# Making the first tile's last expert queries inside its own gather stage, with their weights kept for the second tile

## The chip, the cores and the metric

One Trainium2 chip; the kernel runs on one of its cores. The metric is the device time of one execution in microseconds. The engines are called PE (TensorE), VectorE (DVE in the profile), ScalarE (ACT), GpSimd (POOL) and SP (SyncE, which only issues transfers here).

## The reference, cut to what matters

A decoder trunk of four layers on 256 tokens of width 1024, all in float32. Each layer is a token mixer (HGRN2, FoX attention, Mamba-2 SSD, HGRN2 again) and then an expert layer called PEER. The mixers are causal, so the second half of the tokens needs the first.

```python
for i in range(DEPTH):                       # 4
    h = h + mixer_i(rmsnorm(h, norm_mix[i]))
    h = h + peer_ffn(rmsnorm(h, norm_ffn[i]), ...)
out = rmsnorm(h, norm_final)

def peer_ffn(h, w_q, sub_keys, u_tab, v_tab):    # blocks of 128 tokens
    q = (xb @ w_q).reshape(128, 8, 2, 128)               # 8 heads, w_q is 1024 x 2048
    s = einsum('mhcd,hckd->mhck', q, sub_keys)           # 2 x 128 scores a head
    # the 16 best of each half, then the 16 best of their 256 sums: 16 of 16384 experts a head
    u, v = u_tab[idx], v_tab[idx]                        # rows of 1024
    act = gelu(einsum('md,mhkd->mhk', xb, u)) * softmax(top_s)
    return einsum('mhk,mhkd->md', act, v)
```

Each token reads 8 x 16 rows of u and of v, so 256 tokens and 4 layers read 1.07 GB of expert rows.

## The kernel before, in words

**Gathers.** The tokens form two tiles of 128. The expert layer of one layer and one tile is a *stage*; there are eight, stage s = 2 x layer + tile. A stage has 64 *pairs* (8 heads x 8). For one pair GpSimd issues two indirect gathers (`fetch`, L1389), each of 128 rows of u and v side by side, 1 MB, into one buffer of 2048 columns. VectorE then multiplies and sums the u half (`dot`), ScalarE forms the gated weight on a diagonal (`gated`, `active`; tile `dg`), and PE adds the weighted v half into the stage's sums (`spread`, L1457; tile `acc`). Then `given_back` returns the two buffers to `ring`, and the next pair's `fetches` issue gathers into whatever `ring` holds.

**Side work.** While stage s gathers, everything that stage s+1 needs is made beside it (`side`, `ready`): the norm, the mixer of the next tile (`hgrn`, `fox`, `ssd`), and the queries and scores of its eight heads (`queries`). So an even stage makes the second tile's mixer of its own layer, and an odd stage the first tile's mixer of the next layer. In each pair the main loop runs one step of the side work after `spread` (`products_`), paced by `SIDE[s]`. Top-16 selection (`route`, VectorE) runs some steps a pair, a few heads ahead of the gathers. What comes before the first gather is called the prelude.

**Weights.** A unit is 1 MB, [128 x 2048]. The program walks through `stream`, the list of all units in the order of use: a mixer's units (20 for HGRN2, 16 for FoX, 32 for SSD), then the eight of the query matrix (`wq0` to `wq3`), for each tile. `loads` issues them on SP's queue in the order of `order`, into one of three raw tiles (`raw`), or into a place of its own (`homes`, used once at the start), or, for units named in `KEEP`, into one of six *kept places* in the tile `arena`. A kept unit is loaded for the first tile and used again for the second.

**Places and gather buffers are one pool.** There are seven gather buffers (`NGB`), and a kept place that holds no unit circulates in `ring` as an eighth to thirteenth. When a kept unit comes due, `look_ahead` asks for its place, and the next pair that gives this buffer back makes it vacant. After the second tile has used a kept unit, its place goes back to `ring`.

**What sets the order.** All engines run their instructions in the order in which the program writes them; the waits are semaphores. A gather waits until the buffer's last reader, PE's weighted sum, is done. A raw load waits until PE has used the raw tile's former unit.

The scores of a tile's eight heads stand in `SS` (2048 columns), 256 columns a head.

Of the kernel before, what the change touches and what calls it, by code (L numbers as in the profile page):

```python
# [11 lines left out]
F32 = mybir.dt.float32  # L12
# [22 lines left out]

KEEP = {"hg": (1, 4, 7, 10, 14, 18), "fox": (1, 3, 5, 7, 9, 11, 14), "ssm": (1, 4, 8, 13, 18, 25)}
NKEPT = 6
# [5 lines left out]

SIDE = (43.3, 34.6, 37.5, 100, 100, 38.6, 38.4, 1.8)
SPAN = 56
# [125 lines left out]
def trunk(ctx: ExitStack, tc: tile.TileContext, d: dict, out: bass.AP):  # L171
# [94 lines left out]

    stream = []
# [6 lines left out]
    homes = {3: GB[0], 17: GB[0], 18: GB[1], 19: GB[2], 20: GB[3], 21: GB[4], 22: GB[5], 23: GB[6],  # L274
             27: mix[:, D:3 * D], 28: mix[:, SPACE:SPACE + UNIT], 30: mix[:, 3 * D:5 * D]}
    order = [0, 1, 2, "rest", *range(3, 10), 22, 10, 11, 12, 23, 13, 14, 15, 16, "x", 17, 20, 18, 21, 19, "keys",
             "factors", 28, 29, 24, "heads", 27, 25, 26, "states"]
    order += range(30, len(stream))
    over = set()
# [6 lines left out]
    def spot(u):  # L286

        if isinstance(u, str):
            return None
        nm, i = stream[u]  # L290
        p = KEEP.get(nm.rstrip("01"), ())
        k = p.index(i) if i in p else len(spots)
        return k if k < len(spots) and (nm, i) not in kept else None

# [25 lines left out]
    def loads():  # L320

        while order:
# [12 lines left out]
            else:  # L335
                nm, i = stream[u]
                places = KEEP.get(nm.rstrip("01"), ())
                keep = i in places
                if keep:
                    k = places.index(i)  # L340
# [27 lines left out]
    def half(nm, use):  # L368

        u, k = divmod(pos[1], 2)  # L370
# [11 lines left out]
    def project(nm, ub, names):  # L382

        for key in names:
            b = pjp.tile([P, 512], F32, name="pj")
            for k in range(4):
                def use(w):
                    for c in range(2):
                        mm(b, xT[:, 2 * k + c], w[:, c], 2 * k + c == 0, 2 * k + c == DC - 1)
                half(nm, use)  # L390
                if k == 3:
                    ub[key] = b
                yield
# [35 lines left out]
    class Plan:  # L429
        def __init__(self):  # L430
            self.slots = {}

        def pe(self, n, f, *a):
# [33 lines left out]

    def weighed(row, q, b):

        c = slice(4 * q, 4 * q + 4)  # L470
        tm(xT[:, c], b, weights[:, 8 * row + 4 * q:8 * row + 4 * q + 4].unsqueeze(2).to_broadcast([P, 4, P]), op=OP.mult)

    def half_turned(row, e):

        turned(h[:, 0, e * 512:(e + 1) * 512], lambda b: weighed(row, e, b))

# [11 lines left out]
    def normed(t, acc, row, xn, alone=False):  # L488
# [44 lines left out]
        if not last:  # L533
            yield from slot(*(lambda q=q: turned(xn[:, es[q]], lambda b: weighed(row, q, b)) for q in range(2)))


    def hgrn(l, t, carry):
# [179 lines left out]
        for q in range(2):  # L717
# [14 lines left out]
            else:  # L732
# [56 lines left out]
    def fox(l, t, carry):  # L789
# [93 lines left out]
        for j in range(8):  # L883
# [3 lines left out]
            p.pe(n + 2, scores_turn, j)  # L887
            p.pe(n + 3, out_heads, j)
        p.halves([16, 17, 21, 22], out_project("fox", [YT[:, i] for i in range(8)], acc))
        yield from p.run(3.0)  # L890
# [3 lines left out]
    def ssd(l, t, carry):  # L894
# [223 lines left out]
        for j, n in enumerate([24, 26, 29, 31]):  # L1118
            p.pe(n, gates_turn, j)
            p.pe(n + 1, group_norm, j)  # L1120
            p.at(n + 1, group_root, j)
            p.at(n + 2, group_scale, j)
        gen2 = out_project("ssm", [XT[:, i] for i in range(16)], acc)
        for n in [31, 32, 33, 34] * 3 + [35, 36] * 2:
# [8 lines left out]
    scored, got, routed = set(), {}, [0]  # L1133

    def queries(s, carry):

        l = s // 2
        ub = {}
        top[0] = FREE[KIND[l]]
# [11 lines left out]
        def score(g):  # L1151
            assert s == 0 or routed[0] > 8 * (s - 1) + 2 * g + 1, (s, g, routed)
            b = bank()
# [8 lines left out]
        def alone():  # L1162
# [4 lines left out]
            for hh in range(2):  # L1167
                e, c = slice(hh * 256, hh * 256 + 256), slice(2 * hh, 2 * hh + 2)

                def products(ks):  # L1170
                    for k in ks:
                        mm(b[:, e], xT[:, k], ws[k // 4][:, k % 4, e], k == 0, k == DC - 1)
                if hh == 0:
# [31 lines left out]
        for n, _ in enumerate(p.run(99)):  # L1205
            yield

            while n % 2 and s and routed[0] < min(8 * s, 8 * s - 6 + len([1 for k in scored if k[0] == s])):
                yield "wait"
# [16 lines left out]
    def route(s, hh):  # L1226
# [14 lines left out]
        ig = wk2.tile([P, 2, TOPK], F32, name="ig")  # L1241
        yield from top16([(sv[:, c], si[:, c], SS[:, hh, c]) for c in range(2)])
        vec.tensor_copy(sf, si)
# [124 lines left out]

    def repeated():

        todo = []
        for g in range(2):
            for e in range(2):
                b = bank()
                for c in range(4):
                    for j in range(2):
                        mm(b[j * 64:j * 64 + 64, c * P:(c + 1) * P], xT[:, 4 * e + c, g * 64:g * 64 + 64], ident, True, True)
                todo.append((XR[:, g, e * 512:(e + 1) * 512], b))
# [152 lines left out]
    next(routing)  # L1531
    for i, (o, b) in enumerate(repeated()):
        act(o, b, AF.Copy, scale=rts[1][:, 3 + i // 2:4 + i // 2])
# [14 lines left out]
    for s in range(STAGES):  # L1548
# [26 lines left out]
        for i in range(64 * s, 64 * s + 64):  # L1575
# [15 lines left out]
            if end:  # L1591
                (_, b), (o, c) = x[2:]
                nc.scalar.copy(x[2][0], b)
                vec.tensor_copy(o, c)
            route_steps(3, i // 8 + 3)
            others()
            products_()
            if i % 64 == 62 and s + 1 < STAGES:
# [3 lines left out]
                others()  # L1602
                x = repeated()
            if i == len(pairs) - 1:
# [24 lines left out]
```

## Time and profile before

| | |
|---|---|
| time, median of 3 runs | 3189.3 us (3189.02 to 3190.45) |
| the profiled execution's own time | 3190.3 us |
| its span | 3188.5 us |
| PE, VectorE, ScalarE, GpSimd busy | 82%, 66%, 48%, 39% of the span |
| bytes moved | 1309.40 MB, of which gathers 1073.81 MB |
| unit loads of query weights | 64 (59 into raw tiles, 5 into `arena`), 1 MB each |
| gathers | 1028 |

The chain of waits follows the work back from the last instruction. Releasers are read from semaphores; where the same helper line (L209 for VectorE, L222 for ScalarE, L247 for PE) serves many operations, the tile's name tells which one it is: `pj` are products with weights, `ps` small products and transposes, `acc` the stage's sums.

### The profile page before, as it was taken

How to read it: one execution, taken by the hardware profiler on the slowest of the kernel's cores; microseconds unless marked ns; L12 is line 12 of the kernel's file. 1: busy time of each engine (PE TensorE's matmuls, PEld its weight loads, DVE VectorE, ACT ScalarE, POOL GpSimd, SP SyncE). 2: the span in 40 equal slices, each digit the busy share in tenths (PEclk: the TensorE clock that was granted, in tenths of full speed). 3: DMA queues.
4: the chain of work that ended last, by engine and by line, in shares of the span. 5: the costliest groups of instructions: out<-in, count | busy, mean ns of one | idle time of the engine just before them, and what ended most of it. 6: DMA issues, size and time to landing. Idle time of an engine off the chain costs nothing.

```text
span 3188.5 us, 31234 instructions
## 1 busy us (share of the span) xinstructions
PE 2630.3 (82%) x8618; PEld 973.5 (31%) x8618; DVE 2114.4 (66%) x5602; ACT 1544.0 (48%) x4403; POOL 1231.8 (39%) x1034
## 2 busy tenths in 40 slices
PE   9889877787788886989878998788887888876666
PEld 4433232232233322334323343222322323221111
DVE  1577747676677756778567886476665767667765
ACT  3454434364345543577335784354443554343343
POOL 0244433343344434333334333342333444444544
PEclk9999988998999998999999999999999999999989
DMA  7899999999999999999999999999999999999997
GB/s 314 357 421 421 421 421 421 400 412 421 420 420 420 421 421 421 419 391 398 421 418 413 421 420 421 421 420 415 393 421 412 420 421 421 421 421 421 421 420 322
DMA packets 181500, 1309.40 MB, mean 411 GB/s; under 512 B 20176, under 2 KB 20688, under 8 KB 22608
## 3 DMA queue, kind: packets, MB, share of 16 engines
q0 software_dynamic: 147776, 1073.81, 81.4%
q1 hardware_dynamic: 33552, 233.59, 17.7%
q8 instruction: 72, 1.18, 0.1%
q14 instruction: 100, 0.82, 0.1%
HBM read 1306.27 MB, written 1.05 MB: 410 GB/s over the span
## 4 chain that ended last, share of the span: by engine, by line
DMA 61%; PE 13%; issue 9%; DVE 8%; ACT 4%; POOL 3%; POOLq 0%; SPq 0%; DVEq 0%; ACTq 0%
DMA arena<-in_uv,ix 61%; DVE arena L209 6%; PE pj L247 5%; PE acc L1457 5%; POOL arena L1389 3%; PE ps L247 2%; ACT L222 1%; ACT dg L222 1%; ACT arena L222 1%; PE ps L251 1%; DMA arena<-in_hg 0%; DVE eq L209 0%; ACT dots L222 0%; DVE si L209 0%; DVE ti L209 0%
## 5 line engine op out<-in xcount | busy, mean ns | idle before, releaser
L1389 POOL DMA_INDIRECT arena<-in_uv,ix x1028 | 1229.7, 1196 | 1939.6 <-PE acc L1457 869.5
L209 DVE SCALAR_TENSOR_TENSOR arena<-arena 128x1024 f32<-128x1024 f32 (+3 forms) x1280 | 1320.1, 1049 | 887.2 <-DMA arena<-in_uv,ix 877.1
L1457 PE MATMUL acc<-arena,dg 128*64 128x512 f32 x4096 | 1458.7, 666 | 534.1 <-ACT dg L222 528.8
L222 ACT ACTIVATE dots<-dots 128x1 f32<-128x1 f32 x1024 | 203.8, 199 | 1368.9 <-DVE arena L209 1368.4
L1457 PEld LDWEIGHTS acc<-arena,dg 128*64 128x64 f32 x4096 | 354.3, 145 | 1460.1 <-ACT dg L222 1061.6
L247 PE MATMUL pj<-raw,arena 128*128 128x512 f32 x1440 | 673.3, 610 | 4.2 <-DVE arena L209 3.2
L222 ACT ACT_TABLE_LOAD x322 | 413.1, 1283 | 7.6 <-DVE fst L209 1.3
L247 PEld LDWEIGHTS pj<-raw,arena 128*128 128x128 f32 x1440 | 262.2, 192 | 411.9 <-issue 387.7
L222 ACT ACTIVATE dg<-dg,dots 128x64 f32<-128x64 f32 x1024 | 356.1, 348 | 33.2
L222 ACT ACTIVATE dg<-m,gs 128x64 f32<-128x64 f32 x1024 | 293.9, 335 | 0.0
L247 PE MATMUL pj<-arena 128*128 128x512 f32 (+1 forms) x496 | 222.2, 591 | 0.2
L247 PE MATMUL ps<-arena 128*128 128x128 f32 (+3 forms) x992 | 131.3, 287 | 1.6 <-ACT arena L1187 1.0
L247 PEld LDWEIGHTS pj<-arena 128*128 128x128 f32 x496 | 90.0, 191 | 126.6 <-issue 122.3
L247 PEld LDWEIGHTS ps<-arena 128*128 128x128 f32 (+2 forms) x992 | 102.3, 167 | 68.0 <-issue 44.6
L251 PE MATMUL ps<-fst,arena 128*128 128x128 f32 x568 | 90.9, 286 | 9.1 <-DVE arena L209 5.2
L251 PEld LDWEIGHTS ps<-fst,arena 128*128 128x128 f32 x568 | 66.8, 145 | 87.7 <-issue 45.5
L222 ACT ACTIVATE arena<-arena 128x512 f32<-128x512 f32 (+3 forms) x132 | 67.7, 554 | 52.7 <-DVE arena L209 50.6
L209 DVE DVE_READ_ACCUMULATOR arena<-arena 128x1 f32 x1024 | 84.9, 83 | 0.0
L209 DVE FIND_INDEX8 si<-sv,arena 128x8 uint32<-128x128 f32 x256 | 69.8, 285 | 0.0
L247 PE MATMUL ps<-cst,arena 128*128 128x128 f32 (+3 forms) x288 | 66.6, 358 | 0.0
L209 DVE MAX8 sv<-arena 128x8 f32<-128x128 f32 x256 | 61.7, 283 | 3.4 <-ACT arena L1191 3.4
L222 ACT ACTIVATE arena<-ps 128x512 f32<-128x512 f32 (+3 forms) x114 | 43.3, 426 | 25.7 <-PE ps L247 25.2
(129 smaller groups left out, 1257.6 us busy)
## 6 DMA issues: line engine op xcount, KB each, us to landing
raw<-in_wq SPq DMA_DIRECT2D x59, 1024.0 KB, 9.1
raw<-in_ssm SPq DMA_DIRECT2D x52, 1024.0 KB, 9.2
raw<-in_hg SPq DMA_DIRECT2D x50, 1024.0 KB, 9.3
raw<-in_fox SPq DMA_DIRECT2D x18, 1024.0 KB, 9.2
arena<-in_hg SPq DMA_DIRECT2D x17, 1024.0 KB, 13.6
arena<-in_uv,ix POOLq DMA_INDIRECT x1028, 19.1
arena<-in_fox SPq DMA_DIRECT2D x7, 1024.0 KB, 13.8
arena<-in_ssm SPq DMA_DIRECT2D x6, 1024.0 KB, 14.3
```

The source lines that it names most:

```text
L209: return getattr(nc.vector, name)(o, *a, **k)
L222: nc.scalar.activation(o, i, f, **k)
L247: nc.tensor.matmul(o, w, m, start=start, stop=stop)
L251: nc.tensor.transpose(o, i, ident)
L1389: nc.gpsimd.indirect_dma_start(o, None, src, bass.IndirectOffsetOnAxis(ap=ix, axis=0))
L1457: nc.tensor.matmul(accs[s][e][g * 64:g * 64 + 64], dg[:, g], v, start=hh == 0 and q == 0, stop=hh == 7 and q == NQ - 1)
```

## The change

A layer's queries of the first tile are split. Heads 0 to 3 are still made a stage early, from query units 0 to 3. Heads 4 to 7 are made in the tile's own (even) stage by a new function `late_queries`, which the three mixers call for the second tile; its products are written into the mixer's steps 4 to 5 and 9 to 10. Query units 4 to 7 are loaded once a layer, in that stage, and stay until the second tile's queries at the stage's end have used them too. They go into kept places 0 to 3, whose mixer units the second tile uses first (`KEEP` now names units 0, 1, 4 and 6 of each mixer for these places); `TAIL` says behind which mixer unit each of the four is loaded.

The late queries need the first tile's normed input until then. It is held in `xA`, the upper half of `SS`, where the scores of heads 4 to 7 would stand. So the late steps wait (`hold`) until heads 0 to 3 are routed; the turned queries and the scores of heads 4 and 5 then take places of routed heads (`place_of`). Late products have the weights as the stationary operand and 128 columns of `xA` as the moving one, and give turned queries without a transpose. The route runs up to one head further ahead, with a fourth step a pair when it is behind. The paces `SIDE` are new numbers.

Place 1: SP's queue around the first gather, before. Behind the first layer's keys, `in_wq` are query units and `in_hg` the second tile's mixer units.

```order
L334 DMA arena<-in_keys 128x2048
L357 DMA arena<-in_hg 128x2048
L357 DMA raw<-in_wq 128x2048
L357 DMA arena<-in_wq 128x2048
L357 DMA raw<-in_wq 128x2048 x2
L357 DMA arena<-in_hg 128x2048
L357 DMA raw<-in_hg 128x2048 x12
```

The same place now:

```order
L346 DMA arena<-in_keys 128x2048
L368 DMA arena<-in_hg 128x2048 x3
L368 DMA raw<-in_hg 128x2048 x2
L368 DMA arena<-in_wq 128x2048 x3
L368 DMA raw<-in_hg 128x2048
L368 DMA arena<-in_wq 128x2048
```

The four query units 4 to 7 moved from behind the keys to behind mixer units of the second tile, into kept places. The first gather stands, in both programs, after the unit loads that need nothing but the prelude: before, the first five loads behind the keys (one `in_hg`, four `in_wq`); now the first two (`in_hg`).

Place 2: SP's queue from the first FoX tile's end to the second tile's (end of stage 1 and stage 2), before:

```order
L357 DMA arena<-in_fox 128x2048
L357 DMA raw<-in_fox 128x2048
L357 DMA raw<-in_wq 128x2048 x8
L357 DMA raw<-in_fox 128x2048 x9
L357 DMA raw<-in_wq 128x2048 x8
L357 DMA raw<-in_ssm 128x2048
```

and now:

```order
L368 DMA arena<-in_fox 128x2048
L368 DMA raw<-in_fox 128x2048 x2
L368 DMA raw<-in_wq 128x2048 x4
L368 DMA raw<-in_fox 128x2048 x3
L368 DMA arena<-in_wq 128x2048 x2
L368 DMA raw<-in_fox 128x2048 x2
L368 DMA arena<-in_wq 128x2048 x2
L368 DMA raw<-in_fox 128x2048 x4
L368 DMA raw<-in_wq 128x2048 x4
```

Sixteen loads of query units a layer have become twelve: four for the first tile, four between the second tile's mixer units into kept places, four for the second tile's first heads.

Place 3: PE at the start of stage 4 (SSD, second tile), from the first mixer product on, before (`acc` is the weighted sum of one pair):

```order
L247 MATMUL pj<-raw,arena 128x512 x4
L1457 MATMUL acc<-arena,dg 64x512 x4
L247 MATMUL pj<-arena 128x512 x4
L247 MATMUL ps<-par,arena 128x32 x8
L1457 MATMUL acc<-arena,dg 64x512 x4
L247 MATMUL pj<-raw,arena 128x512 x4
L251 MATMUL ps<-fst,arena 128x128 x4
L1457 MATMUL acc<-arena,dg 64x512 x4
```

and now, from the third pair of that stretch on:

```order
L253 MATMUL ps<-fst,arena 128x128 x4
L249 MATMUL pj<-arena 128x128 x16
L1530 MATMUL acc<-arena,dg 64x512 x4
L249 MATMUL pj<-raw,arena 128x512 x4
L249 MATMUL pj<-arena 128x128 x16
L1530 MATMUL acc<-arena,dg 64x512 x4
L249 MATMUL pj<-arena 128x512 x4
L253 MATMUL ps<-fst,arena 128x128 x4
L249 MATMUL ps<-arena 128x128 x4
L1530 MATMUL acc<-arena,dg 64x512 x4
```

Between two weighted sums there now stand, four times in an even stage, 16 late products of 128 columns beside the mixer's four of 512, and the late scores (`ps`) behind them.

The diff, cut to its core:

```diff
-KEEP = {"hg": (1, 4, 7, 10, 14, 18), "fox": (1, 3, 5, 7, 9, 11, 14), "ssm": (1, 4, 8, 13, 18, 25)}
+KEEP = {"hg": (0, 1, 4, 6, 12, 17), "fox": (0, 1, 4, 6, 9, 13, 11), "ssm": (0, 1, 4, 6, 15, 24), "wq": (4, 5, 6, 7)}
+TAIL = ((6, 4), (6, 5), (8, 6), (9, 7))
-SIDE = (43.3, 34.6, 37.5, 100, 100, 38.6, 38.4, 1.8)
+SIDE = (47, 31, 43.5, 100, 100, 35.2, 45, 1.8)
...
+    xA = at_["SS"][:, 1024:2048].rearrange("p (c t) -> p c t", c=DC)
...
-            stream += [(nm, i) for i in range(UNITS[KIND[l] if KIND[l] != "ssd" else "ssm"])]
-            stream += [("wq%d" % l, i) for i in range(8)]
+            for i in range(UNITS[KIND[l] if KIND[l] != "ssd" else "ssm"]):
+                stream.append((nm, i))
+                for behind, k in TAIL if t else ():
+                    if behind == i:
+                        tails[l, k] = len(stream)
+                        stream.append(("wq%d" % l, k))
+            stream += [("wq%d" % l, i) for i in range(8 if t else 4)]
...
+                while n in self.holds and routed[0] < self.holds[n]:
+                    yield "wait"
...
+        if t:
+            late_queries(p, l, 4, 9)
...
+    def place_of(s, hh):
+        return hh if s % 2 or hh not in (4, 5) else hh - 4
+    def late_queries(p, l, *starts):
...
+        def products(g, n):
+            if n == 0:
+                bs[g] = pjp.tile([P, 512], F32, name="pj")
+            ws = [raws[tails[l, 2 * g + i]][0].rearrange("p (k n) -> p k n", k=4) for i in range(2)]
+            for k in range(DC):
+                mm(bs[g][:, n * P:(n + 1) * P], ws[k // 4][:, k % 4, n * P:(n + 1) * P], xA[:, k], k == 0, k == DC - 1)
...
+        for g, n in zip((2, 3), starts):
+            for i in range(4):
+                p.pe(n + i // 2, products, g, i)
+            if g == 2:
+                p.hold(n, 8 * s + 4)
+            p.at(n + 1, evac, g)
+            p.pe(n + 2, score, g)
...
-        gs = range(0 if s else 1, 4)
-        p.halves(range(2 * len(gs)), project("wq%d" % l, ub, gs))
+        gs = range(0 if s else 1, 4 if s % 2 else 2)
+        p.halves(range(2 * len(gs)), project("wq%d" % l, ub, gs, x))
...
-            route_steps(3, i // 8 + 3)
+            route_steps(3 + (routed[0] < i // 8 + 3), i // 8 + 4)
```

More of the change, by code (lines that the diff above doesn't have):

```diff
@@ L270, in trunk @@
         for t in range(2):
-            stream += [(nm, i) for i in range(UNITS[KIND[l] if KIND[l] != "ssd" else "ssm"])]
-            stream += [("wq%d" % l, i) for i in range(8)]
-    homes = {3: GB[0], 17: GB[0], 18: GB[1], 19: GB[2], 20: GB[3], 21: GB[4], 22: GB[5], 23: GB[6],
-             27: mix[:, D:3 * D], 28: mix[:, SPACE:SPACE + UNIT], 30: mix[:, 3 * D:5 * D]}
+            for i in range(UNITS[KIND[l] if KIND[l] != "ssd" else "ssm"]):
[5 more added lines that the diff above has]
+            stream += [("wq%d" % l, i) for i in range(8 if t else 4)]
+    main = [u for u in range(len(stream)) if u not in tails.values()]
+    homes = {4: GB[0], 16: GB[0], 18: GB[1], 19: GB[2], 20: GB[3], 21: GB[4], 22: GB[5], 23: GB[6],
+             26: mix[:, SPACE:SPACE + UNIT], 27: mix[:, D:3 * D], 29: mix[:, 3 * D:5 * D]}
     order = [0, 1, 2, "rest", *range(3, 10), 22, 10, 11, 12, 23, 13, 14, 15, 16, "x", 17, 20, 18, 21, 19, "keys",
-             "factors", 28, 29, 24, "heads", 27, 25, 26, "states"]
-    order += range(30, len(stream))
+             "factors", 24, 25, 26, "heads", 27, 28, "states", 29, 30, 33, 34, 31, 32]
+    order += range(35, len(stream))
     over = set()
@@ L289, in spot, with place @@
             return None
+        k = place(u)
+        return k if k is not None and k < len(spots) and stream[u] not in kept else None
+    def place(u):
         nm, i = stream[u]
-        p = KEEP.get(nm.rstrip("01"), ())
-        k = p.index(i) if i in p else len(spots)
-        return k if k < len(spots) and (nm, i) not in kept else None
+        p = KEEP["wq" if nm[:2] == "wq" else nm.rstrip("01")]
+        return p.index(i) if i in p else None
     def given_back(b):
@@ L336, in loads @@
                 nm, i = stream[u]
-                places = KEEP.get(nm.rstrip("01"), ())
-                keep = i in places
+                k = place(u)
+                keep = k is not None
                 if keep:
-                    k = places.index(i)
                     r = spots[k] if k < NKEPT else mix[:, MIX - UNIT:]
@@ L431, in __init__, with hold @@
             self.slots = {}
+            self.holds = {}
+        def hold(self, n, until):
+            self.holds[n] = until
         def pe(self, n, f, *a):
@@ L466, in turned, with weighed @@
         later(lambda: use(b))
-    def weighed(row, q, b):
+    def weighed(row, t, q, b):
         c = slice(4 * q, 4 * q + 4)
-        tm(xT[:, c], b, weights[:, 8 * row + 4 * q:8 * row + 4 * q + 4].unsqueeze(2).to_broadcast([P, 4, P]), op=OP.mult)
+        tm((xA if row >= DEPTH and not t else xT)[:, c], b, weights[:, 8 * row + 4 * q:8 * row + 4 * q + 4].unsqueeze(2).to_broadcast([P, 4, P]), op=OP.mult)
     def half_turned(row, e):
-        turned(h[:, 0, e * 512:(e + 1) * 512], lambda b: weighed(row, e, b))
+        turned(h[:, 0, e * 512:(e + 1) * 512], lambda b: weighed(row, 0, e, b))
     def half_squared(rt, e, xn):
@@ L533, in normed @@
         if not last:
-            yield from slot(*(lambda q=q: turned(xn[:, es[q]], lambda b: weighed(row, q, b)) for q in range(2)))
+            while not t and row >= DEPTH and routed[0] < 16 * (row - DEPTH):
+                yield "wait"
+            yield from slot(*(lambda q=q: turned(xn[:, es[q]], lambda b: weighed(row, t, q, b)) for q in range(2)))
     def hgrn(l, t, carry):
@@ L1133, in trunk, with turned_queries, evac, score @@
     scored, got, routed = set(), {}, [0]
+    def place_of(s, hh):
+        return hh if s % 2 or hh not in (4, 5) else hh - 4
+    def late_queries(p, l, *starts):
+        s = 2 * l
+        root = 1.0 if s else rts[1][:, 2:3]
+        bs = {}
+        def products(g, n):
[4 more added lines that the diff above has]
+                mm(bs[g][:, n * P:(n + 1) * P], ws[k // 4][:, k % 4, n * P:(n + 1) * P], xA[:, k], k == 0, k == DC - 1)
+            if n == 3:
+                for i in range(2):
+                    raws.pop(tails[l, 2 * g + i])
+        def turned_queries(g):
+            return at_["SS"][:, (g - 1) * 512:g * 512].rearrange("p (g t) -> p g t", g=4)
+        def evac(g):
+            assert routed[0] >= 8 * s + 4, (s, g, routed)
+            nc.scalar.copy(turned_queries(g), bs.pop(g).rearrange("p (g t) -> p g t", g=4))
+        def score(g):
+            b, qt = bank(), turned_queries(g)
+            for i in range(4):
+                mm(b[:, i * P:(i + 1) * P], qt[:, i], keys[:, 4 * g + i], True, True)
+            def use():
+                h0 = place_of(s, 2 * g)
+                act(SS[:, h0:h0 + 2], b.rearrange("p (h c k) -> p h c k", h=2, c=2), AF.Copy, scale=root)
+                scored.update((s, 2 * g + i) for i in range(2))
+            later(use)
+        for g, n in zip((2, 3), starts):
+            for i in range(4):
+                p.pe(n + i // 2, products, g, i)
[3 more added lines that the diff above has]
+            p.pe(n + 2, score, g)
     def queries(s, carry):
         l = s // 2
+        x = xT if s % 2 else xA
         ub = {}
@@ L1206, in queries @@
             yield
-            while n % 2 and s and routed[0] < min(8 * s, 8 * s - 6 + len([1 for k in scored if k[0] == s])):
+            while n % 2 and s and routed[0] < min(8 * s, 8 * s - 6 + 4 * (s % 2) + len([1 for k in scored if k[0] == s])):
                 yield "wait"
@@ L1241, in route @@
         ig = wk2.tile([P, 2, TOPK], F32, name="ig")
-        yield from top16([(sv[:, c], si[:, c], SS[:, hh, c]) for c in range(2)])
+        yield from top16([(sv[:, c], si[:, c], SS[:, place_of(s, hh), c]) for c in range(2)])
         vec.tensor_copy(sf, si)
@@ L1531, in trunk @@
     next(routing)
-    for i, (o, b) in enumerate(repeated()):
+    for i, (o, b) in enumerate(repeated(xA)):
         act(o, b, AF.Copy, scale=rts[1][:, 3 + i // 2:4 + i // 2])
```

22 lines of the change are left out of this document (13 added, 9 removed).

## The prediction

> **What bounds the kernel now.** I read the page first, then the busy time by stage, then the waits of GpSimd's queue.
>
> ```profile
> span 3188.5 us, 31234 instructions
> PE 2630.3 (82%) x8618; PEld 973.5 (31%) x8618; DVE 2114.4 (66%) x5602; ACT 1544.0 (48%) x4403; POOL 1231.8 (39%) x1034
> GB/s 314 357 421 421 421 421 421 400 412 421 420 420 420 421 421 421 419 391 398 421 418 413 421 420 421 421 420 415 393 421 412 420 421 421 421 421 421 421 420 322
> DMA packets 181500, 1309.40 MB, mean 411 GB/s; under 512 B 20176, under 2 KB 20688, under 8 KB 22608
> q0 software_dynamic: 147776, 1073.81, 81.4%
> q1 hardware_dynamic: 33552, 233.59, 17.7%
> DMA 61%; PE 13%; issue 9%; DVE 8%; ACT 4%; POOL 3%; POOLq 0%; SPq 0%; DVEq 0%; ACTq 0%
> ```
>
> The two queues' packets fill 81.4 + 17.7 = 99% of the 16 DMA engines' span, and 61% of the chain that ended last is gathers. Most slices stand at 421 GB/s, so that is the ceiling here: 1309.4 MB at 421 GB/s are 3110 us, and the other 78 us are slices in which the transfers ran short. A unit of 1,048,576 bytes is worth 2.49 us. VectorE, ScalarE and GpSimd are busy 66, 48 and 39%; TensorE, at 82%, is the only engine near the transfers.
>
> Where the transfers run short is seen by stage (rows of windows; columns: length, busy time of PE, weight load, VectorE, ScalarE, GpSimd, then granted clock, DMA share, GB/s). The edges are the first dot product of each stage.
>
> ```profile
> 119.00:511.00 392.00, 331.92 (x1089) 122.56 (x1087) 256.99 (x683) 181.07 (x524) 159.12 (x129) 0.95 1.01 421
> 511.00:888.00 377.00, 301.60 (x978) 107.84 (x976) 249.25 (x677) 174.69 (x536) 142.85 (x128) 0.92 1.01 414
> 888.00:1262.00 374.00, 306.56 (x1056) 117.75 (x1056) 253.86 (x675) 180.95 (x539) 155.89 (x132) 0.93 1.01 421
> 1262.00:1684.00 422.00, 363.79 (x1242) 144.31 (x1242) 299.01 (x821) 240.34 (x637) 150.88 (x126) 0.94 1.00 410
> 1684.00:2101.00 417.00, 364.04 (x1266) 147.29 (x1266) 298.07 (x814) 234.30 (x625) 157.19 (x132) 0.95 1.01 419
> 2101.00:2488.00 387.00, 318.05 (x1020) 112.04 (x1020) 253.16 (x653) 183.76 (x525) 143.77 (x126) 0.95 1.00 412
> 2488.00:2862.00 374.00, 315.71 (x1017) 110.49 (x1016) 254.26 (x655) 183.40 (x523) 159.85 (x133) 0.95 1.01 421
> ```
>
> Time lost in a stage is (421 - GB/s) / 421 of its length: stage 1 loses 6.3 us, stage 3 11.0, stage 5 8.3; stages 0, 2 and 6 lose nothing, stage 4 2.0. The odd stages are those in which places are taken from the gathers for kept units. Counted along the program, at pair 32 of stages 0 to 6 the gathers circulate in 11, 7, 13, 7, 12, 7, 12 buffers. So seven buffers lose 6 to 11 us a stage, eleven to thirteen about nothing, at a similar load of PE. One such loss close up, in stage 5 (waits in 2228 to 2250, then the timeline):
>
> ```profile
> POOL arena L1389 <- PE acc L1457: 17.2, 4, 8.2
> 2230.80 4.17 PE L247 MATMUL pj<-arena 128*128 128x512 f32 x8
> 2231.14 1.72 POOL L1389 DMA_INDIRECT arena<-in_uv,ix  x1 [8.21 <-PE acc L1457]
> 2244.74 0.33 SPq L357 DMA_DIRECT2D raw<-in_hg  x1
> ```
>
> The gather waits 8.21 us for a buffer that PE's weighted sum must release; no weight load is issued until 2244.74, since PE is working on a kept unit, which frees no raw tile. With neither queue supplied, the transfers stop.
>
> **The change, part by part.** *Transfers.* 64 loads of query units become 48: 16 x 2.49 = 39.8 us. Not all of it counts:
>
> ```profile
> 100.00:120.00 20.00, 17.31 (x116) 11.94 (x115) 14.61 (x68) 8.54 (x16) 7.00 (x6) 1.00 0.44 165
> 109.69 1.08 POOL L1389 DMA_INDIRECT arena<-in_uv,ix  x1 [108.00 <-DVE ix L209]
> 87.59 0.91 SPq L357 DMA_DIRECT2D raw<-in_wq  x2
> 122.95 0.33 SPq L357 DMA_DIRECT2D arena<-in_hg  x1
> ```
>
> The first gather waits for the first head's indices at 109.69, while the queues stand half empty (165 GB/s). Before it, the old order loads five units behind the keys, the new order two; the other unit loads fall from 186 to 173. So three of the sixteen are taken from a stretch that waits for compute anyway, and 13 x 2.49 = 32.4 us count, 12 of them in stages 1, 3 and 5 (four each). The prelude itself I cost at nothing: PE's work sets it, and its order is the same.
>
> *PE.* Per moved group of two heads, 8 products of 512 columns, 4 transposes and 4 scores become 32 products of 128 columns and 4 scores. Each stands twice in the trace:
>
> ```profile
> L247 PE MATMUL pj<-raw,arena 128*128 128x512 f32 x1440 | 673.3, 610 | 4.2 <-DVE arena L209 3.2 <-ACT arena L695 0.7 <-DMA raw<-in_hg 0.3
> L251 PE MATMUL ps<-fst,arena 128*128 128x128 f32 x568 | 90.9, 286 | 9.1 <-DVE arena L209 5.2 <-ACT arena L222 2.8 <-ACT arena L952 1.1
> L247 PE MATMUL ps<-arena 128*128 128x128 f32 x480 | 73.7, 289 | 1.0 <-ACT arena L1187 1.0
> ```
>
> Busy time over count: 0.468 us for 512 columns, 0.160 for a transpose, 0.154 for 128 columns. An odd stage loses 16 x 2 x 0.468 + 8 x 0.160 + 8 x 2 x 0.154 = 18.7 us of PE; stages 2, 4 and 6 gain 72 x 2 x 0.154 = 22.1; stage 0, which made these groups already, gains 3.4. From the same row, the trace prices four 128-column products at 1.31 times one of 512. The Trainium skill (TensorE: Matmul & The Clock Gate, Back-to-back issue gap) gives 81 ns against 131 ns sustained, a ratio of 2.47; by that the late products would cost an estimated 37 us a stage instead of 19.7, and the sum would be about the slower rival's. The trace disagrees, so the rows stand.
>
> *Buffers.* This is the term on the other side. Kept places now hold query units from early in an even stage to its end: at pair 32 the counts become 7, 7, 8, 7, 8, 7, 8. No row shows an even stage with so few. Below, the loss is nothing (today's even stages); above, each even stage loses what the odd one of its mixer loses: HGRN2 8.3 twice, FoX 6.3, SSD 11.0 less the 2.0 it has, 31.9 in all. It can't be a gain, since fewer buffers supply no transfer. I take 20, nearer the upper end, because the counts lie at the odd stages' 7 and 8 for most of an even stage and PE has more to do there; not all of it, because the late query units are transfers in flight just when kept units are worked on.
>
> *Odd stages* have 18.7 us less of PE in front of their weighted sums; of their 25.6 us I give back 3 (ends 0 and 13, half).
>
> *The rest at nothing.* ScalarE saves 8 copies out of PSUM beside 48% busy time. VectorE's extra route step per pair, when routing is behind, moves work and adds none; uncovered it would delay one dot product by under a microsecond a pair. The hold on the late queries is met twice in the program, both in stage 0, where side work pauses for a pair. The routes of heads 4 to 7 come later in an even stage, and GpSimd's gathers wait for their indices; along the program head 4 of these stages is routed by pair 18 to 25 and first gathered for at pair 29, and the smallest lead, four pairs, is eight gathers or 20 us at the ceiling, so the route hides behind gathers already queued. If that cover went, GpSimd would stand still for what VectorE is late. SP's loads of units 4 to 7 stand behind the reader of the place; behind them wait the mixer's next raw loads, which is part of the 20.
>
> Sum: -32.4 + 20 - 3 = -15.4. The profiled execution took 3190.3 us (1.8 around the span) and gives 3174.9; the median of the runs is 1.0 lower, so 3174.
>
> **Rivals.** *Full saving.* The even stages lose nothing and the odd ones a little less: 3189 - 32 - 3 = 3154. For it: stage 0 ran on seven buffers for its first 15 pairs, inside a row at 421 GB/s. The Trainium skill (Perfetto Trace Analysis, Identifying the Most-Contended Engine) holds matmul busy time a poor measure and weight-load time the better; by that rule, with 115.5 of 307 us in the third row below, PE has room for all of it. Against: the loss at 2231 lies in a stage whose weight loading, 112.0 of 387 us, is no denser.
>
> *Nothing left.* The even stages copy the odd ones in full: -32.4 + 31.9 - 3 = -3.5, 3186, within 0.2% (6.4 us), about what a measurement can tell from no change.
>
> *Slower: PE becomes the bound where side work is dense,* the first 48 or so pairs of stages 2, 4 and 6:
>
> ```profile
> 888.00:1180.00 292.00, 248.46 (x840) 97.01 (x840) 207.29 (x560) 148.66 (x438) 125.30 (x106) 0.94 1.01 421
> 1262.00:1582.00 320.00, 281.63 (x950) 113.05 (x951) 241.32 (x673) 201.31 (x515) 113.30 (x93) 0.95 0.99 407
> 1684.00:1991.00 307.00, 278.43 (x974) 115.51 (x976) 240.25 (x664) 195.35 (x503) 118.60 (x100) 0.97 1.01 419
> 2488.00:2773.00 285.00, 244.07 (x756) 84.79 (x756) 195.82 (x504) 146.17 (x404) 118.35 (x100) 0.97 1.01 421
> ```
>
> With 22.1 us more, PE is busy 270.6 of 292, 300.5 of 307 and 266.2 of 285. If it can't be filled beyond the 91% that it reaches in stage 4 now, these stretches need 298, 331 and 293 us: +38, so 3189 + 38 - 32 = 3195. It decides from +32.4, that is, if PE's idle share can't fall under 8.6%. For it: stage 3 loses most at 88%. Against: PE's idle time is mostly waiting for data that the transfers bring late, so it shrinks as PE fills.
>
> **How the numbers follow.** Part given back (3165 to 3182) 0.42; full saving 0.26; nothing left 0.18; slower 0.14. Faster by over 0.2%: 0.68; within: 0.18; slower: 0.14. The forecast is the first's 3174, its own range 3165 to 3182. For 8 in 10 the range takes in the full saving to 3153 and the even stages' whole loss with part of the slower case, to 3190.
>
> **What will show it.** Right: the page's bytes fall by 16.8 MB to 1292.6; the rate stays 421; stages 1, 3 and 5 shorten by some 11 us each; stages 2, 4 and 6 drop under 421 GB/s, with GpSimd waiting for PE's weighted sum and no load in flight. PE busy rises by 10 to 17 us. Wrong: even stages stay at 421 (full saving), or PE is above 95% in 1684 to 1991's counterpart with the rate near 400 (slower). The first gather moving off 109.7 would upset the count of 13.

## The result and the profile after

The changed kernel takes 3157.6 us (median of 4 runs, 3157.22 to 3158.15), the kernel before 3189.9 us beside it (3189.02 to 3190.46): ratio 0.9899, 95% interval 0.9882 to 0.9916, that is 32.3 us less. The forecast was 15.4 us less. The sign was right, and the forecast gain was less than half of the measured one; the time lies 4 us above the rival "full saving" (3154).

The page of the kernel after: span, engines, rate in 40 slices, packets, the two queues (their packets' time as a share of 16 engines' span at the end), and the chain that ended last by engine.

```profile
span 3155.5 us, 31905 instructions
...
PE 2600.9 (82%) x8970; PEld 998.7 (32%) x8970; DVE 2111.5 (67%) x5602; ACT 1546.5 (49%) x4406; POOL 1222.5 (39%) x1034
...
GB/s 327 302 421 421 420 421 420 416 401 421 419 414 418 421 421 421 418 400 411 415 421 411 404 419 422 420 419 416 410 414 418 412 421 410 421 421 421 421 421 336
...
DMA packets 179198, 1292.65 MB, mean 410 GB/s; under 512 B 19920, under 2 KB 20432, under 8 KB 22352
...
q0 software_dynamic: 147776, 1073.81, 82.4%
q1 hardware_dynamic: 31248, 216.82, 16.7%
...
DMA 52%; DVE 14%; issue 14%; PE 8%; POOL 4%; ACT 2%; POOLq 0%; DVEq 0%; ACTq 0%
```

The ceiling is still 421 GB/s, and the two queues still fill 82.4 + 16.7 = 99% of the engines' span. 16.75 MB are gone, all from q1, the unit loads. Less of the chain is gathers (52% after 61%) and more of it is VectorE and issue, but the transfers remain the bound.

The busy time by stage after, columns as before; the edges are again the first dot product of each stage.

```profile
119.00:512.00 393.00, 332.10 (x1177) 130.60 (x1175) 260.47 (x702) 189.16 (x532) 149.56 (x130) 0.92 1.01 421
512.00:876.00 364.00, 284.64 (x920) 98.62 (x920) 248.09 (x675) 174.08 (x532) 155.47 (x128) 0.92 1.01 415
876.00:1257.00 381.00, 317.49 (x1200) 132.32 (x1200) 258.81 (x698) 182.42 (x545) 151.72 (x131) 0.93 1.01 419
1257.00:1660.00 403.00, 345.42 (x1186) 134.01 (x1186) 297.27 (x816) 238.15 (x633) 152.67 (x127) 0.95 1.00 413
1660.00:2083.00 423.00, 372.15 (x1410) 161.59 (x1410) 298.23 (x812) 235.11 (x628) 152.53 (x131) 0.95 1.01 416
2083.00:2456.00 373.00, 302.28 (x964) 104.82 (x964) 248.77 (x637) 177.35 (x514) 151.31 (x128) 0.91 1.01 414
2456.00:2831.00 375.00, 321.27 (x1160) 127.00 (x1160) 258.31 (x676) 187.53 (x531) 148.01 (x132) 0.95 1.01 418
2831.00:3155.00 324.00, 212.55 (x526) 49.93 (x526) 206.34 (x480) 122.24 (x421) 153.72 (x122) 0.92 0.97 401
```

The last row is stage 7. Put beside the rows before:

| stage | 0 | 1 | 2 | 3 | 4 | 5 | 6 | sum |
|---|---|---|---|---|---|---|---|---|
| length before, us | 392 | 377 | 374 | 422 | 417 | 387 | 374 | |
| length after | 393 | 364 | 381 | 403 | 423 | 373 | 375 | |
| difference | +1 | -13 | +7 | -19 | +6 | -14 | +1 | -31 |
| unit loads more or fewer, x 2.49 us | 0 | -12.5 | +5.0 | -14.9 | +5.0 | -14.9 | 0 | -32.4 |
| time lost before, (421 - GB/s) / 421 | 0 | 6.3 | 0 | 11.0 | 2.0 | 8.3 | 0 | 27.6 |
| time lost after | 0 | 5.2 | 1.8 | 7.7 | 5.0 | 6.2 | 2.7 | 28.6 |

The loads of a stage are counted along the program. A rate is printed to 1 GB/s, so a lost time is known to about half a microsecond a stage within one profile; between two profiles, stages that an edit does not touch differ by up to 3 us (see `b_lend2`). The table tells the result: the bytes give 32.4 us back, and the time in which the transfers run short is what it was, 28.6 us after 27.6. It only lies elsewhere: the odd stages lose 19.0 instead of 25.6, the even ones 9.5 instead of 2.0. The forecast had 17 us more of it. (The last stage, which loses 15.4 us after 18.6, and the end give the remaining 2 us of the span's 33.)

One of the places where stage 4 now runs short, 1750 to 1780 us, as a row of windows:

```profile
1750.00:1780.00 30.00, 28.04 (x144) 17.30 (x144) 23.19 (x72) 19.23 (x49) 6.58 (x7) 0.94 0.98 393
```

The timeline of the same place, GpSimd's queue and SP's (start, us; in brackets the idle time before and what ended it):

```profile
1770.36 0.94 POOL L1462 DMA_INDIRECT arena<-in_uv,ix  x1 [11.23 <-DVE gt L211]
...
1751.28 38.23 SPq L368 DMA_DIRECT2D raw<-in_ssm  x4
```

It is like the place at 2231 before: a gather waits (there 8.21 us for PE, here 11.23 us for VectorE, `gt` being a tile of the route), SP gets only four loads away in 38 us, since their raw tiles wait for PE, and the rate falls to 393.

### The profile page after: what moved, and what is told of

Same layout as the page of the kernel before. It is cut to its first block, busy times and chain, and to the rows that moved or that the text cites. A ratio compares the mean times of both kernels' runs of the same rounds, so it can differ in the third digit from the quotient of the medians.

```text
span 3155.5 us, 31905 instructions
## 1 busy us (share of the span) xinstructions
PE 2600.9 (82%) x8970; PEld 998.7 (32%) x8970; DVE 2111.5 (67%) x5602; ACT 1546.5 (49%) x4406; POOL 1222.5 (39%) x1034
## 3 DMA queue, kind: packets, MB, share of 16 engines
q0 software_dynamic: 147776, 1073.81, 82.4%
q1 hardware_dynamic: 31248, 216.82, 16.7%
## 4 chain that ended last, share of the span: by engine, by line
DMA 52%; DVE 14%; issue 14%; PE 8%; POOL 4%; ACT 2%; POOLq 0%; DVEq 0%; ACTq 0%
DMA arena<-in_uv,ix 52%; DVE arena L211 9%; POOL arena L1462 4%; PE acc L1530 4%; PE pj L249 3%; PE ps L249 2%; DVE eq L211 1%; ACT L224 1%; DVE af L211 1%; ACT dg L224 1%; ACT arena L224 0%; DVE gs L211 0%; DVE si L211 0%; DVE ti L211 0%; PE ps L253 0%
## 5 line engine op out<-in xcount | busy, mean ns | idle before, releaser
L1462 POOL DMA_INDIRECT arena<-in_uv,ix x1028 | 1220.4, 1187 | 1915.9 <-PE acc L1530 1128.6
L1530 PE MATMUL acc<-arena,dg 128*64 128x512 f32 x4096 | 1432.1, 667 | 527.1 <-ACT dg L224 524.5
L249 PE MATMUL pj<-raw,arena 128*128 128x512 f32 x1184 | 555.1, 610 | 4.9 <-DMA raw<-in_ssm 2.3
L249 PE MATMUL pj<-arena 128*128 128x512 f32 (+2 forms) x1136 | 347.1, 455 | 4.8 <-ACT arena L976 1.8
L249 PEld LDWEIGHTS pj<-raw,arena 128*128 128x128 f32 x1184 | 215.2, 192 | 343.2 <-issue 320.2
L249 PEld LDWEIGHTS pj<-arena 128*128 128x128 f32 x1136 | 174.4, 193 | 181.8 <-issue 163.6
L253 PE MATMUL ps<-fst,arena 128*128 128x128 f32 x536 | 83.9, 282 | 7.2 <-DVE arena L211 4.9
L224 ACT ACTIVATE arena<-ps 128x512 f32<-128x512 f32 (+4 forms) x120 | 46.7, 435 | 25.4 <-PE ps L249 24.7
## 6 DMA issues: line engine op xcount, KB each, us to landing
arena<-in_uv,ix POOLq DMA_INDIRECT x1028, 16.4
```

The costliest lines, as they stand in the source:

```text
L224: nc.scalar.activation(o, i, f, **k)
L249: nc.tensor.matmul(o, w, m, start=start, stop=stop)
L253: nc.tensor.transpose(o, i, ident)
L1462: nc.gpsimd.indirect_dma_start(o, None, src, bass.IndirectOffsetOnAxis(ap=ix, axis=0))
L1530: nc.tensor.matmul(accs[s][e][g * 64:g * 64 + 64], dg[:, g], v, start=hh == 0 and q == 0, stop=hh == 7 and q == NQ - 1)
```

## The experiments

Each run is compared with the kernel before, run beside it on the same chip. "Against after" is the difference of the two gains (after: -32.3 us); since the kernel before itself had medians from 3187.4 to 3189.9 us on different chips, such a difference is good to a microsecond or two.

### The bytes

**a_reload**: the kernel after, but units 4 to 7 are loaded again, in place, for the second tile.

```diff
-                elif not keep or (nm, i) not in kept:
+                elif not keep or (nm, i) not in kept or nm[:2] == "wq":
```

> The changed kernel, but query units 4 to 7 are loaded a second time for the second tile into the place where they already lie: 16 loads of 1 MB more, all inside even stages, with the late queries, buffers and paces as they are. If the gain is bytes at 421 GB/s, the time rises by 16 x 2.49 = 39.8 us to 3197, more than the change gained, since the old order had three of these loads before the first gather. If idle transfer time in the even stages can take them up, it rises by less: the 9.5 us that they now lose at most come off, 3188.

3196.2 us, ratio 1.0021 (1.0011 to 1.0030): +38.9 against after. The page's bytes:

```profile
DMA packets 181502, 1309.43 MB, mean 410 GB/s; under 512 B 20176, under 2 KB 20688, under 8 KB 22608
```

With the bytes of the kernel before (1309.40 MB) and everything else as after, the gain is gone. 16 loads in the stages of gathers cost 2.43 us each, against 2.49 by the ceiling. So the saving is the bytes, and an added MB there is paid in full.

**a_keys4**: the kernel after, with the first layer's keys loaded four times, three loads more ahead of the first gather.

```diff
-                nc.sync.dma_start(keys, d["keys"][0].rearrange("p (g k) -> p g k", g=16))
+                for _ in range(4):
+                    nc.sync.dma_start(keys, d["keys"][0].rearrange("p (g k) -> p g k", g=16))
```

> The changed kernel with the first layer's keys loaded four times over, 3 MB more before the first gather. The prediction's count of 13 instead of 16 says that three loads there are free: 0 to 2 us more. If loads before the first gather cost as much as later ones, +7.5 us; if they delay the keys, the first gather moves by as much.

3156.0 us, ratio 0.9896 (0.9880 to 0.9913): -1.3 against after. Its timeline, SP's queue and the first gather:

```profile
66.51 29.88 SPq L347 DMA_DIRECT2D arena<-in_keys  x4
...
108.86 1.08 POOL L1463 DMA_INDIRECT arena<-in_uv,ix  x1 [107.17 <-DVE ix L211]
```

The same gather in the timeline of the kernel after:

```profile
109.43 1.09 POOL L1462 DMA_INDIRECT arena<-in_uv,ix  x1 [107.74 <-DVE ix L211]
```

The four loads of the keys keep SP's queue for 30 us, and the first gather starts no later, since it waits for the indices. Three MB there cost nothing. So the change's three fewer loads ahead of the first gather were rightly not counted: 13 and not 16.

**a_early** and **a_early3**: the kernel after, with two (three) of the raw loads that stand behind the first gather moved ahead of it.

```diff
-             "factors", 24, 25, 26, "heads", 27, 28, "states", 29, 30, 33, 34, 31, 32]
-    order += range(35, len(stream))
+             "factors", 24, 25, 26, "heads", 27, 28, 33, 34, 36, "states", 29, 30, 31, 32, 35]
+    order += range(37, len(stream))
```

(`a_early` moves 33 and 34 only.)

> The changed kernel with two unit loads (units 7 and 8 of the second tile, into raw tiles) moved ahead of the point that waits for the prelude's states, so that they go out before the first gather, where the transfers stand half empty. If a transfer there is free and one behind it costs 2.49 us, the time falls by 5.0 us to 3152.6. If the losses elsewhere absorb it, no change.

3152.6 us, 0.9884 (0.9868 to 0.9901): -4.8 against after.

> As a candidate: three unit loads instead of two ahead of the first gather, into the third raw tile too. At 2.49 us a load 3150.1; no further gain if the third raw tile comes free only after the first gather.

3147.6 us, 0.9872 (0.9856 to 0.9889): -7.9 against after. In its timeline the three loads (`raw<-in_hg`) are issued at 87, 22 us ahead of the first gather, which again doesn't move:

```profile
86.99 1.62 SPq L368 DMA_DIRECT2D raw<-in_hg  x3
...
109.09 1.09 POOL L1462 DMA_INDIRECT arena<-in_uv,ix  x1 [107.40 <-DVE ix L211]
```

The same price from the other side: 2.4 and 2.6 us for each load that leaves the gather stages for the half-empty queues of the prelude. The program has three raw tiles, and no run moved a fourth load. Together with `a_early3s` below, which can't be told from it, this is the fastest version of the study.

### The buffers

**b_ring7**: the kernel *before*, but its kept places are never lent to the gathers, which have seven buffers in all stages (ten in the last).

```diff
-        if k in wanted:
-            wanted.remove(k)
+        if k is not None:
+            wanted.discard(k)
```

> The kernel before with one edit: a kept place never circulates as a gather buffer, so all stages up to the seventh run on seven buffers; transfers and order of work stay. My prediction's buffer term says stages 0, 2, 4 and 6 then lose what the odd ones do, up to 31.9 us in all: 3210 to 3222. The rival, that seven buffers cost an even stage little and that the odd stages' losses come from elsewhere (places taken away, loads waiting for them), says 3189 to 3200, with the odd stages' 25.6 us of loss falling.

3191.8 us, ratio 1.0007 (0.9997 to 1.0016): 2.2 us more than before. By stage:

```profile
121.00:512.00 391.00, 331.26 (x1094) 121.51 (x1092) 257.59 (x685) 181.16 (x525) 155.87 (x129) 0.97 1.01 418
512.00:889.00 377.00, 303.80 (x976) 108.59 (x976) 248.37 (x675) 174.29 (x535) 150.84 (x129) 0.90 1.01 416
889.00:1265.00 376.00, 309.46 (x1056) 118.60 (x1056) 253.27 (x673) 180.99 (x538) 142.77 (x129) 0.93 1.00 412
1265.00:1682.00 417.00, 362.63 (x1242) 144.94 (x1242) 299.00 (x823) 240.91 (x637) 149.90 (x128) 0.95 1.01 417
1682.00:2100.00 418.00, 361.77 (x1267) 145.62 (x1266) 298.54 (x814) 234.32 (x625) 151.08 (x129) 0.96 1.01 413
2100.00:2488.00 388.00, 317.68 (x1020) 111.56 (x1020) 254.07 (x653) 184.11 (x526) 149.91 (x130) 0.95 1.01 420
2488.00:2860.00 372.00, 311.97 (x1016) 110.17 (x1016) 253.70 (x653) 183.31 (x523) 147.43 (x129) 0.97 1.01 416
2860.00:3188.00 328.00, 209.29 (x526) 48.67 (x526) 215.01 (x522) 125.15 (x425) 154.36 (x127) 0.94 0.97 402
```

Stage 7 in the kernel before:

```profile
2862.00:3188.00 326.00, 214.98 (x526) 50.84 (x526) 214.72 (x522) 125.10 (x425) 154.95 (x123) 0.91 0.96 397
```

The even stages lose 2.8, 8.0, 7.9 and 4.4 us, 23 in all, about what I had put on them. But the odd stages, which had seven buffers in both kernels at mid-stage, fall from 25.6 to 9.4 us. Together that is 32.5 against 27.6, and stage 7 loses 14.8 us instead of 18.6. So lending up to six more buffers is worth about 2 us (2.2 by the time, 1.2 by the rows), not 20: of the 21 us that the even stages gain by it, 16 are paid in the odd ones and 4 in the last. The edit does one thing more: since a place is free whenever it holds no unit in use, no load of a kept unit waits for a place to come back.

**b_lend2**: the kernel before, places lent in stages 2 and 3 only.

```diff
+    now = [0]
...
-        if k in wanted:
-            wanted.remove(k)
+        if k in wanted or k is not None and now[0] not in (2, 3):
+            wanted.discard(k)
...
+        now[0] = s
```

> The kernel before with seven gather buffers throughout, except that in stages 2 and 3 kept places circulate as they did (up to 13 in stage 2, taken back in stage 3). If lent buffers only put a loss off, stage 2's loss of 8 us goes to about 0 and stage 3's rises from 4 us to about 11, the other stages stay as with seven buffers throughout, and the time stays within 4 us of 3191. If the odd stages' loss has another cause, stage 2's 8 us are gained (3183) and stage 3 stays near 4.

3188.3 us, ratio 1.0004 (0.9994 to 1.0013). Stages 2, 3 and 4:

```profile
886.00:1263.00 377.00, 308.93 (x1056) 117.53 (x1056) 254.51 (x675) 180.74 (x539) 158.97 (x132) 0.93 1.01 421
1263.00:1680.00 417.00, 363.39 (x1242) 144.35 (x1242) 299.10 (x823) 240.44 (x637) 147.90 (x126) 0.94 1.00 411
1680.00:2098.00 418.00, 362.17 (x1266) 147.71 (x1266) 298.28 (x812) 234.51 (x627) 153.56 (x129) 0.96 1.01 414
```

Against the rows of `b_ring7`, stage 2 falls from 8.0 to 0 and stage 3 rises from 4.0 to 9.9; stage 4, not lent to, stands at 7.0 (7.9). Stages 5 and 6, which neither kernel lends to, differ by 2.8 and 1.8 us between the two profiles; the moves of stages 2 and 3 are larger. So the loss of stage 3 is not simply the price of seven buffers: most of it appears when stage 2 is given more and the places are called back in stage 3. Whether stage 3 makes up for transfers that stage 2 put off or pays for the calling back, this run does not separate. PE's work is the same in all three kernels.

**a_ring7** and **a_ring6**: the kernel after, once with the edit of `b_ring7`, once with one gather buffer taken out of circulation when the fourth head is routed, so that six to eight circulate.

```diff
-        else:
+        elif not (b is GB[6] and routed[0] > 3):
             ring.append(b)
```

> The changed kernel with kept places that never circulate: seven gather buffers in every stage but the last, where today seven to nine circulate. In the kernel before, the same edit cost the even stages 21 us and gave the odd ones 16 back. If the changed kernel's even stages lose only 9.5 us because one or two places still circulate in their second half, their loss rises to 20 us or more. If it is because their query units' loads are in flight while kept units are worked on, it stays near 10 and the odd stages' 19.1 falls to about 10: 3147 to 3152.

3157.7 us, 0.9905 (0.9888 to 0.9921): +2.2 against after, the same small worth of lending. The row of stage 6, where the loss rises most:

```profile
2457.00:2832.00 375.00, 322.60 (x1160) 128.95 (x1160) 257.30 (x674) 187.28 (x530) 144.20 (x128) 0.94 1.00 411
```

The even stages lose 18.6 us instead of 9.5, stage 6 alone 8.9 instead of 2.7, and the odd ones 15.3 instead of 19.0. Of the two cases expected, this is nearer the first: the one or two places that still circulate in the changed kernel are a good part of why its even stages lose so little. But the time hardly shows it, since the odd stages and the last one (11.5 instead of 15.4) lose less.

> The changed kernel with one gather buffer fewer from the first stage on (six to eight circulate instead of seven to nine). If seven buffers are just enough, six cost some 2.5 us of cover per pair where side work is dense: +30 us or more, 3190 and above, with the DMA share under 0.97 in all stages. If the number of buffers hardly matters here, within 5 us of 3158.

3163.4 us, 0.9918 (0.9901 to 0.9934): +6.1 against after; the stages 0 to 6 lose 38.6 us instead of 28.6. It is neither of the two cases expected, but one buffer fewer costs more than all that are lent above seven.

### PE

**a_late2**: the kernel after; the late products are computed twice, the second time over the first.

```diff
-            for k in range(DC):
+            for k in 2 * list(range(DC)):
```

> The changed kernel with the late products computed twice (the second pass starts the sum anew): some 15.6 us of PE more in each even stage, 62 in all, no transfer and no buffer changed. If the transfers bind and PE has room, the time rises by under 10 us. If PE is all but the bound in the dense part of the even stages (294 of 318 us busy in stage 4), it rises by 30 us or more.

3166.6 us, 0.9929 (0.9912 to 0.9945): +9.2 against after. The late products in PE's groups by form, first of the kernel after, with the products of 512 columns from `arena` beside them (behind the bar the busy time and the mean of one):

```profile
L249 PE MATMUL pj<-arena 128*128 128x512 f32 x592 | 277.2, 612 | 4.8 <-ACT arena L976 1.8 <-DVE arena L211 1.4 <-DMA arena<-in_hg 0.9
...
L249 PE MATMUL pj<-arena 128*128 128x128 f32 x512 | 62.5, 278 | 0.0
```

And of `a_late2`:

```profile
L249 PE MATMUL pj<-arena 128*128 128x128 f32 x1024 | 121.7, 278 | 0.0
```

Its stages 1, 3, 4 and 5 as rows of windows; stage 4 is the densest:

```profile
512.00:875.00 363.00, 286.12 (x920) 98.22 (x920) 247.72 (x678) 173.94 (x532) 142.72 (x127) 0.91 1.01 417
1255.00:1660.00 405.00, 343.85 (x1186) 134.48 (x1186) 302.39 (x836) 238.71 (x636) 155.86 (x127) 0.95 1.01 416
1660.00:2090.00 430.00, 383.42 (x1538) 175.65 (x1538) 298.13 (x812) 234.91 (x630) 152.35 (x131) 0.95 0.99 407
2090.00:2462.00 372.00, 301.50 (x964) 104.65 (x964) 249.08 (x637) 177.38 (x515) 151.92 (x128) 0.91 1.01 418
```

59 us more of late products cost 9 us by the medians; the profiled execution, at 3162.3 us, is the fastest of the four. PE's whole busy time rises by only 32 us (2633.1 after 2600.9), since that of the weighted sums falls from 1432.1 to 1408.8. Stage 4 loses 14.3 us instead of 5.0 (430 us long, 423 after). PE is not the bound, even with 383 of 430 us busy, but it is no longer quite free there. The odd stages, which have no late products, lose 10.9 us instead of 19.0, while the even ones lose 24.2 instead of 9.5: the same give and take as with the buffers, with no buffer changed.

### The smaller parts of the change

**a_route_old** takes back the deeper route, **a_side_old** the paces of the side work.

```diff
-            route_steps(3 + (routed[0] < i // 8 + 3), i // 8 + 4)
+            route_steps(3, i // 8 + 3)
```

```diff
-SIDE = (47, 31, 43.5, 100, 100, 35.2, 45, 1.8)
+SIDE = (43.3, 34.6, 37.5, 100, 100, 38.6, 38.4, 1.8)
```

> The changed kernel with the old route rule (three steps a pair, three heads ahead instead of four). If the deeper route is what kept the losses of the even stages at 9.5 instead of 20 us, the time rises by 5 to 12 us, with GpSimd waiting for indices. If it only moves VectorE's work, it stays within 3 us of 3158.

3157.2 us, 0.9898 (0.9882 to 0.9915): -0.1 against after. GpSimd's gathers wait about 240 us in all for tiles of the route (108 of them for the first gather), against 310 us in the kernel after and 240 before; the time does not follow these waits.

> The changed kernel with the old paces SIDE (43.3, 34.6, 37.5, 100, 100, 38.6, 38.4). If the new paces keep the even stages' losses low, side work now runs late in stages 0, 2 and 6, has to be forced through at their end, and the time rises by 10 to 30 us. If the paces matter little, within 4 us of 3158.

3156.0 us, 0.9896 (0.9880 to 0.9913): -1.3 against after. Neither part matters for the time. The split by stage does move: the even stages lose 14.1 us and the odd ones 13.5, instead of 9.5 and 19.0, and the sum is 27.6 again.

### Looking for more

**a_early7** is `a_early` with the edit of `b_ring7`; **a_ahead** is `a_early` with `AHEAD` 10 instead of 5, so that kept places are asked back ten units ahead; **a_early3s** is `a_early3` with the old paces.

> As a candidate: places that never circulate, and the two unit loads ahead of the first gather. If both are independent, 5.0 us less than the kernel with only the first edit.

3151.1 us, 0.9889 (0.9873 to 0.9906): -4.4 against after, within half a microsecond of `a_early`.

> As a candidate: two unit loads early, and places asked back ten units ahead instead of five. If the odd stages' 19.1 us of loss come from unit loads that stand in SP's queue behind a place not yet given back, they fall by 5 us or more (3147); if they come from the smaller number of buffers, they rise, since places leave the gathers sooner (3153 to 3158).

3151.3 us, 0.9887 (0.9871 to 0.9904): -4.2, no gain over `a_early`. The odd stages lose 16.4 us, in `a_early` 18.1: unit loads that wait behind a place not yet given back explain little of it here.

> As a candidate: three unit loads ahead of the first gather, and the old paces SIDE, which alone were 1.6 us below the changed kernel. If both hold and add up, 1.6 us below the kernel with the three loads; if the paces' gain was noise, the same as that one.

3147.0 us, 0.9875 (0.9859 to 0.9892): -8.1, no gain over `a_early3` that this could tell.

## Why the prediction was half of the result

**Transfers, -32.4: right.** The bytes, the ceiling of 421 GB/s and the count of 13 all held. `a_reload` gives the price of a load (2.43 us), `a_keys4` shows that those ahead of the first gather are free, and the first gather stayed at 109.43 (109.69 before). Only the places were off: the prediction put four loads fewer on each odd stage, but along the program 5, 6 and 6 leave stages 1, 3 and 5, and stages 2 and 4 take two more each. So the odd stages became 13, 19 and 14 us shorter, not some 11 each.

**Buffers, +20: this is the step that failed.** It said that even stages with seven or eight buffers would lose most of what the odd ones lose, and nothing in the sum came back for it. Measured: +7.5 (2.0 to 9.5), and the odd stages lose 6.6 less. The fault was in the reading that led to it, "seven buffers lose 6 to 11 us a stage, eleven to thirteen about nothing". The rows compared stages that follow each other as if each were on its own. `b_ring7` gives all of them seven: the even stages do lose 21 us more, about what the term said, but the odd ones lose 9.4 us, not 25.6. `b_lend2` lends in stages 2 and 3 alone, and stage 3's loss comes with it. So lending mostly moved a loss from one stage to the next. A change that takes lent buffers away costs the even stages something and saves the odd ones nearly as much, and only the first half stood in the sum. How the loss passes from one stage to the next was not traced and stays open; that it moves with the lending is shown by the two runs, and `a_late2` and `a_side_old` show that it moves for other reasons too.

**Odd stages, -3: too small.** Measured -6.6 (25.6 to 19.0). I tied it to PE's 18.7 us less work; `b_ring7` moves this loss by 16 us with PE's work unchanged. The sum took 3, though half of its own upper end, 13, is 6.5; that 6.5 comes near the measured value is luck. How much of the 6.6 is PE's relief and how much is give and take, no run tells apart: the old paces alone move this loss by another 5.5 us (`a_side_old`).

**The two together** were +17 in the sum and are about +1. This is 16 of the 17 us between the forecast gain, 15.4, and the result.

**PE: the busy time went the other way.** Forecast +10 to +17, measured -29.4 (2630.3 to 2600.9). By the form rows, 512 late products take 62.5 us, 0.122 each and not 0.154: that is 16 us of it. Another 27 us is the weighted sum, which has the same 4096 products in both kernels. Its group by form, before:

```profile
L1457 PE MATMUL acc<-arena,dg 128*64 128x512 f32 x4096 | 1458.7, 666 | 534.1 <-ACT dg L222 528.8 <-DMA arena<-in_uv,ix 2.7
```

and after:

```profile
L1530 PE MATMUL acc<-arena,dg 128*64 128x512 f32 x4096 | 1432.1, 667 | 527.1 <-ACT dg L224 524.5
```

In `a_late2` it is 1408.8. The same work can differ by 27 us and more in busy time, with the mean of one product unchanged; a forecast of busy time to 10 us was finer than the measure.

**The rival "slower"** fell: it needed PE unable to fill beyond 91% in stage 4's dense part. The same 48 pairs of stage 4 after:

```profile
1660.00:1978.00 318.00, 293.53 (x1123) 132.37 (x1124) 232.56 (x627) 194.25 (x504) 113.86 (x98) 0.96 1.00 414
```

PE is busy 92% of it, and 94% in `a_late2` (306.7 of 326 us). The rival had 298, 331 and 293 us for these stretches of stages 2, 4 and 6; they take 276, 318 and 289. Its price of 38 us counted busy time as if none of it could be taken up in PE's waits. The Trainium skill (Perfetto Trace Analysis, Identifying the Most-Contended Engine) holds matmul busy time a poor measure because matmuls are pipelined. This case agrees: the same weighted sums differ by up to 50 us in busy time between the kernels.

**"GpSimd waiting for PE's weighted sum", the sign that I named, was there and misled.** The waits of GpSimd's gathers for PE and for transfers (total, times, longest, in us), before:

```profile
POOL arena L1389 <- PE acc L1457: 869.5, 355, 10.3
POOL arena L1389 <- DMA arena<-in_uv,ix: 306.6, 173, 4.5
```

and after:

```profile
POOL arena L1462 <- PE acc L1530: 1128.6, 387, 8.7
POOL arena L1462 <- DMA arena<-in_uv,ix: 74.1, 74, 2.0
```

Those for PE grew by 259 us in total, while the transfers lost 1 us more. Most of this looks like another name for the same waiting: those that end with a transfer shrank by 233 us, and GpSimd's whole idle time before its gathers went from 1939.6 to 1915.9 us. With that much waiting the transfers still stand at or near 421 GB/s in most stretches, so a wait of the gather queue by itself does not price a loss; in the two places seen close up, SP's loads waited too. The Trainium skill (Perfetto Trace Analysis, Optimization Strategy) says that gaps which repeat can mean too few buffers; here one buffer fewer costs something (`a_ring6`, +6.1), and going down from thirteen to seven hardly anything (`b_ring7`, +2.2).

**At nothing:** the route and the paces, rightly so for the time (`a_route_old`, `a_side_old`). But the route does not always hide behind gathers already queued, as the prediction argued: at 1770 a gather waits 11.23 us for it by the profile, and the rate falls. The old depth shortens these waits and leaves the time unchanged, so the depth sets nothing. No run tests ScalarE's copies alone; its busy time hardly changes (1546.5 us after 1544.0).

**Open:** what sets the remaining 28 us that stages 0 to 6 lose. It rises by 10 with a buffer fewer and by 7 with 59 us more of late products, so more than one thing feeds it; asking for places earlier (`a_ahead`) does not clearly lower it.

## What to carry to other kernels

When transfers are the bound, price a change by its bytes at the sustained rate first, and count the loads that lie where the queue is half empty as free; a load that can be moved there is worth its whole duration (2.5 us for 1 MB here). Do not read the cost of a buffer from two neighbouring stages with different counts: what one stage gains by it, the next may lose, so sum the lost time over all stages, and test by fixing the count in all. And a long wait at the head of a gather queue is no loss as long as the rate of transfers in that stretch stands at its ceiling.

## What the hardware showed that was not expected

Four products of 128 columns cost hardly more than one of 512: 4 x 0.122 = 0.488 us against 277.2 / 592 = 0.468, a ratio of 1.04 in busy time where the prediction had 1.31 from a row of small products (`ps`). The late products stand 16 at a time, the scores beside them four; whether that makes the difference, no run shows. And the busy time of 4096 identical weighted sums was 1458.7, 1432.1 and 1408.8 us in three kernels, with a mean of 666 to 667 ns each time.
